# A two-layer network on one core: a third block of seven products in three feed-forward stages, with one of its weight sums added by transfers

## The chip, the cores and the metric

The kernel runs on one core of a Trainium2 chip. The metric is device time in microseconds (us) of one execution. The core's engines each run their own list of instructions in order and wait for one another through semaphores: TensorE (PE, matrix products, with its weight loads shown apart as PEld), VectorE (DVE), ScalarE (ACT), GpSimd (POOL) and SyncE (SP), which here issues the DMA transfers.

## The reference, cut to what matters

The kernel computes two layers over 256 tokens of width 1024, all in fp32. Each layer is a feed-forward part, a mixer, and a second feed-forward part, each followed by a residual sum and a layer norm:

```python
def swiglu(x, w_in, w_out):                     # w_in 1024 x 5632, w_out 2816 x 1024
    gate, up = jnp.split(x @ w_in, 2, axis=-1)
    return (jax.nn.silu(gate) * up) @ w_out

for layer in range(2):
    h = layer_norm(ALPHA * h + 0.5 * swiglu(h, ffn_w_in[layer, 0], ffn_w_out[layer, 0]), ...)
    h = layer_norm(ALPHA * h + mix(h), ...)     # layer 0: gated delta rule and state space; layer 1: sparse attention
    h = layer_norm(ALPHA * h + 0.5 * swiglu(h, ffn_w_in[layer, 1], ffn_w_out[layer, 1]), ...)
```

So there are six stages. Stages 1, 3, 4 and 6 are feed-forward, and these are what the change is about. Stage 2 is the hybrid mixer and stage 5 the sparse attention.

## The kernel before, in words

**Products.** An fp32 product is made of three TensorE products in the reduced type fp32r: a value is split into a high part (`hi`, a copy that rounds) and a low part (`lo`, the value less its high part), and hi·hi, hi·lo and lo·hi are summed (`mm3`). Weights come from DRAM into one of four `raw` buffers (128 partitions x 2048 values, 1 MB). ACT, sometimes DVE as a CAST, copies each half of it (128x1024) into a `whi` buffer, and DVE subtracts to make `wlo`. These, the results `g` and other intermediates such as `e` (128x1024) come from a pool of 36 buffers of one size, in which weights have a quota of 12 to 24. The activations of a stage lie in an `x` buffer of 128x4096 values (2 MB). There are two of these, so during a stage one of them is spare until the stage's layer norm writes the next stage's activations.

**A feed-forward stage.** The 2816 hidden columns are 11 steps of 256. The first step or two (`NT`) are done token by token. The rest follow a string, `PATTERN`, in which a letter stands for:

- R, one plain step (`proj_two`). Four banks (ps, ps, mp, mp) take 8 matmuls of 128x512 and 8 of 128x256 each: 32 and 32. DVE and ACT then add the two halves of each bank into `sg`, apply SiLU, multiply, and split the result into `g`.
- S, two steps at once (`block`), as a fast 2x2 block product with seven products instead of eight. Each product is 12 matmuls of 128x512, 84 in all. The left factors are blocks and sums of blocks of the activations (`sums_of_tokens`, made once for a stage, tiles `sgh` and `sgl`). The right factors are b11, b21, b22 and four weight sums T1 to T4, each in two halves h = 0 and 1 of 128x1024. T1 = b11 + b12, T3 = b12 + b22, T2 = T1 + b22 and T4 = T2 + b21, each added in place (T3 over b12, the others over b11); the signs lie in the activation sums. For each half DVE adds, then the sum is split into `whi` and `wlo` like any weight. Four banks A, B (tag ps) and C, D (tag mp) gather the products, `e1` and `e2` hold the partial results, and 8 transposes (128x128) bring the result into the form of `g`.

After each letter the out-projection of the step before goes into four `acc` banks: for a block 48 matmuls of 128x512.

Stage 1 (NT = 1) has the string "RRRSRSRR", and stages 3, 4 and 6 (NT = 2) have "RSRRSRR".

**Order.** The code writes operations in program order into a `Plan`. A list scheduler in it (`order`) decides the order of each engine's instructions, with a price for each operation, priorities, quotas and a table `ORDER` of corrections. So an edit of `block` moves instructions on every engine. All instructions are issued by one line (L559 before, L564 after), so profile rows are told apart by the names of their tiles. A number after a name in an order row says which tile it is.

Of the kernel before, what the change touches and what calls it, by code (L numbers as in the profile page):

```python
# [9 lines left out]
F32 = mybir.dt.float32  # L10
F32R = mybir.dt.float32r
I32 = mybir.dt.int32
AF = mybir.ActivationFunctionType
OP = mybir.AluOpType
# [18 lines left out]
    "ps": (2, "PSUM"), "mp": (2, "PSUM"), "acc": (4, "PSUM"),  # L33
}

QUOTAS = {"M": None, "S": (8, 8), "Z": (4, 4), "L": (4, 4), "G": (4, 4), "P": (5, 5), "Q": (5, 5), "D": (4, 4), "W": (12, 24)}

KEPT = ("L", "G")

# [6 lines left out]

KEEP_WARM = 5500

PATTERN = {1: "RRRSRSRR", 2: "RSRRSRR"}


def H3(t, h):
# [120 lines left out]
class Plan:  # L173
# [76 lines left out]
    def price(self, op, eng, fn, args, kw):  # L250
# [13 lines left out]
                return 63.0 if N <= 64 else max(146.0, N * 0.896)  # L264
            return N * 1.7708 if N > M else 235.0 if N == M else 224.0
        if fn == "dma_start":
            return 60.0
# [60 lines left out]
    def order(self, caps):  # L328
        ops = self.ops
        for op in ops:  # L330
            if op.fn == "dma_start":
                a = op.args[0] if isinstance(op.args[0], V) else op.args[1]
                op.nbytes = (a.p1 - a.p0) * a.ids.size * 4
                if isinstance(op.args[1], V) and op.args[1].t.space == "DRAM":
# [12 lines left out]
            op.table = self.TABLES.get(getattr(op.args[2], "name", str(op.args[2])) if op.fn == "activation" else "")  # L347
# [8 lines left out]
        ready = {e: [] for e in engs}  # L356
        free = {e: 0.0 for e in engs}
        table = None
        dma_free = 0.0
        partial = heavy = False  # L360
        run = 0
        last = None
# [68 lines left out]
        while left:  # L431
# [79 lines left out]
                port = st + c  # L511
            op.start = st
            if fn == "dma_start":
                dma_free = max(dma_free, st + 1300) + op.nbytes / 360.0
                op.end = dma_free + 600
                free[e] = st + c
            else:
                op.end = st + c
                free[e] = st + c
# [63 lines left out]
class K:  # L583
    NT = 2
    LAG = 5

    def __init__(self, plan, ins, caps):
        self.nc = self.plan = plan
# [327 lines left out]
    def block(self, st, w, c0, c1):  # L916

        nc, V = self.nc, self.nc.vector
        raw = []
        for h in range(2):  # L920
            tiles = [self.plan.tile("raw", [P, 2048], F32, "raw", stream="W") for r in range(2)]
            for r, t in enumerate(tiles):
                for e, c in enumerate((c0, c1)):
                    k = 4 * r + 2 * h
                    nc.sync.dma_start(t[:, e * 1024:(e + 1) * 1024].rearrange("p (k n) -> p k n", k=2),
                                      w[:, k:k + 2, c:c + 512])
            raw.append(tiles)
        A, B, C, D = (self.bank(tag) for tag in ("ps", "ps", "mp", "mp"))
        e1, e2 = self.m4(1024, "e1"), self.m4(1024, "e2")
        lh, rh = slice(0, 512), slice(512, 1024)  # L930

        def form(n, h):
            (r1, r2), u, v = raw[h], slice(0, 1024), slice(1024, 2048)
            left = r1[:, u]
            if n == "T1":
                V.tensor_tensor(left, left, r1[:, v], OP.add)
            elif n == "T3":
                V.tensor_tensor(r1[:, v], r1[:, v], r2[:, v], OP.add)
            elif n == "T2":
                V.tensor_tensor(left, left, r2[:, v], OP.add)  # L940
            elif n == "T4":
                V.tensor_tensor(left, left, r2[:, u], OP.add)
            src = {"b21": r2[:, u], "b22": r2[:, v], "T3": r1[:, v]}.get(n, left)
            hi, lo = self.m4(1024, "whi", "W", F32R), self.m4(1024, "wlo", "W", F32R)
            self.split(hi, lo, src)
            return hi, lo
# [6 lines left out]
                    self.mm3(bank, st[a][2 * h + k], (hi[:, cs], lo[:, cs]), start and h + k == 0, stop and h + k == 2,  # L953
                             **({} if start else {"skip_group_check": True}))
        product(A, "a11", "b11", True, True)
        product(B, "5", "T1", True, True)
        self.copy(e1[:, lh], A)
        product(A, "a12", "b21", False, True)
        self.copy(e1[:, rh], B)
        product(C, "7", "T3", True, True)  # L960
        nc.scalar.activation(e2[:, lh], A, AF.Silu)
        V.tensor_tensor(e1[:, rh], e1[:, rh], C, OP.subtract)
        product(B, "3", "b22", False, True)
        product(D, "2", "T2", True, True)
# [3 lines left out]
        V.tensor_tensor(e2[:, rh], B, e1[:, lh], OP.add)  # L968
        V.tensor_tensor(e2[:, lh], e2[:, lh], e2[:, rh], OP.mult)
        V.tensor_tensor(e1[:, rh], e1[:, rh], e1[:, lh], OP.add)  # L970
# [15 lines left out]
    def ffn(self, l, j, x, then):  # L986
# [62 lines left out]
        def flush(keep):  # L1049
            while len(todo) > keep:  # L1050
                f, g, wo = todo.pop(0)
                out_mm(0, f, g, wo)
                if f >= NF - self.LAG:
                    late.append((f, g, wo))
                else:
                    out_mm(1, f, g, wo)
        st = None
        s = NT
        for n, kind in enumerate(PATTERN[NT]):
            if n == 3:  # L1060
                self.mark = len(self.plan.ops) - 1
            if kind == "S":
                if st is None:
                    st = self.sums_of_tokens(x)
                go = self.block(st, w_in, s * 256, DFF + s * 256)
                next(go)
                wo = self.unit_rows(w_out, 2 * s, 2, 0, D) + self.unit_rows(w_out, 2 * s + 2, 2, 0, D)
# [6 lines left out]
            if s == NT:  # L1074
                for m in range(NT):
                    wo = self.unit_rows(w_out, 2 * m, 2, 0, D)
                    todo += [(2 * m + e, gts[2 * m + e], wo[e]) for e in range(2)]
# [1040 lines left out]
    def run(self, stages):  # L2118
# [53 lines left out]
SPLIT, SHIFT = 4900, 10  # L2172
HOMES = [38, 1389, 3572, 4905, 6238, 7367]
ORDER = {
# [98 lines left out]
```

## Time and profile before

| | us |
|---|---|
| runs (three) | 1091.36, 1091.8, 1095.76; median 1091.8 |
| profiled execution | 1091.2, with a span of 1089.5 |
| PE busy | 1076.1 (99%), 6132 matmuls |
| DVE busy | 968.5 (89%), 1471 instructions |
| ACT busy | 634.7 (58%), 1066 instructions |
| POOL busy | 49.1 (5%), 78 instructions |
| stage 1, hybrid mixer | 0 to 194, 197 to 424.7 |
| stages 3 and 4 | 424.7 to 605.3, 605.3 to 787.5 |
| sparse attention, stage 6 | 787.5 to 906.6, 906.6 to 1083.7 |

The span is what the profiler saw from the first to the last instruction; the profiled execution's own time is 1.7 us longer. The stages are cut at their layer norms. Matmuls are pipelined, so the mean of one matmul in a group of the page (390 ns) is longer than the pitch at which they follow each other. The prediction goes by pitches.

### The profile page before, as it was taken

To read this page: it belongs to the slowest core of one execution; us is meant where nothing else is said; L and a number is where in the kernel's file an instruction comes from. 1 tells how busy PE (TensorE), PEld (TensorE's weight loads), DVE (VectorE), ACT (ScalarE), POOL (GpSimd) and SP (SyncE) were. 2 spreads that over 40 slices of the span, in tenths; PEclk is the share of its full clock that TensorE was granted. 3 is DMA by queue.
4 is the path that set the end of the run, shared out by engine and by line. 5 is a ranking of instruction groups with operands and counts; after the bars stand their busy time and mean duration, and the time that the engine had idled before them with its cause. 6 is when DMAs were issued, how large, how long until landed. Compare 5 with 4: busy or idle time off the path is not lost.

```text
span 1089.5 us, 16005 instructions
## 1 busy us (share of the span) xinstructions
PE 1076.1 (99%) x6132; PEld 907.0 (83%) x6132; DVE 968.5 (89%) x1471; ACT 634.7 (58%) x1066; POOL 49.1 (5%) x78
## 2 busy tenths in 40 slices
PE   8999999999999999999999999999999999999997
PEld 6888888788999788888888888888887678888886
DVE  7999996888979899999995999897888999999965
ACT  5665673489788544555573655564375765655540
POOL 0000300001000110000000000010001000000000
PEclk9999999999999999999999999999999999999999
DMA  9919395633652383458394609378464145285541
GB/s 331 325 31 335 116 341 171 215 116 104 213 191 100 116 302 114 164 178 285 109 340 169 222 11 332 132 239 276 155 197 152 59 136 192 79 282 182 208 140 39
DMA packets 135799, 201.52 MB, mean 185 GB/s; under 512 B 10077, under 2 KB 95530, under 8 KB 135722
## 3 DMA queue, kind: packets, MB, share of 16 engines
q1 hardware_dynamic: 135722, 200.50, 54.2%
q8 instruction: 48, 0.79, 0.3%
q14 instruction: 29, 0.24, 0.1%
HBM read 197.18 MB, written 1.07 MB: 182 GB/s over the span
## 4 chain that ended last, share of the span: by engine, by line
PE 93%; DVE 3%; DMA 2%; ACT 1%; issue 1%; SPq 0%; DVEq 0%; ACTq 0%
PE ps L559 38%; PE acc L559 33%; PE mp L559 22%; DMA raw<-in_ffn_w_in_dram 1%; DVE arena L559 1%; DVE wlo L559 1%; DVE qs L559 0%; SPq L559 0%; DMA arena<-in_ssd_a_log_dram 0%; ACT whi L559 0%; DVE h L559 0%; DVE P L559 0%; DVE F L559 0%; ACT L559 0%; DVE g L559 0%
## 5 line engine op out<-in xcount | busy, mean ns | idle before, releaser
L559 DVE TENSOR_TENSOR wlo<-raw,whi 128x1024 fp32r<-128x1024 f32 (+1 forms) x396 | 469.0, 1213 | 10.2 <-ACT whi L559 7.7
L559 ACT ACTIVATE whi<-raw 128x1024 fp32r<-128x1024 f32 (+1 forms) x356 | 361.1, 1050 | 136.6 <-DMA raw<-in_ffn_w_in_dram 55.2
L559 PE MATMUL acc<-whi,g 128*128 128x512 f32 x704 | 223.3, 390 | 0.0
L559 PE MATMUL ps<-whi,x 128*128 128x512 f32 (+1 forms) x608 | 169.9, 386 | 1.3 <-DVE whi L559 1.3
L559 PE MATMUL ps<-x,whi 128*128 128x512 f32 (+1 forms) x720 | 159.2, 343 | 1.0 <-ACT cv L559 0.9
L559 PEld LDWEIGHTS acc<-whi,g 128*128 128x128 f32 x704 | 132.3, 188 | 26.7
L559 PE MATMUL acc<-wlo,g 128*128 128x512 f32 x352 | 137.4, 390 | 0.0
L559 PEld LDWEIGHTS ps<-x,whi 128*128 128x128 f32 x720 | 123.0, 189 | 17.2 <-ACT cv L559 2.4
L559 PEld LDWEIGHTS ps<-whi,x 128*128 128x128 f32 x608 | 109.7, 188 | 23.7 <-DVE whi L559 2.1
L559 PE MATMUL ps<-x,wlo 128*128 128x256 f32 x544 | 98.9, 284 | 0.0
L559 PE MATMUL ps<-wlo,x 128*128 128x512 f32 (+1 forms) x304 | 95.0, 385 | 0.5 <-DVE wlo L559 0.5
L559 PEld LDWEIGHTS ps<-x,wlo 128*128 128x128 f32 x544 | 81.1, 191 | 2.2 <-issue 0.2
L559 PE MATMUL mp<-x,whi 128*128 128x512 f32 x336 | 80.8, 390 | 0.2 <-DVE g L559 0.2
L559 ACT ACTIVATE sg<-ps 128x256 f32<-128x256 f32 x56 | 21.3, 380 | 95.6 <-PE ps L559 95.5
L559 PEld LDWEIGHTS acc<-wlo,g 128*128 128x128 f32 x352 | 66.2, 188 | 12.8
L559 PEld LDWEIGHTS mp<-x,whi 128*128 128x128 f32 x336 | 62.9, 188 | 13.6 <-DVE g L559 0.6
L559 DVE TENSOR_TENSOR sg<-ps,sg 128x256 f32<-128x256 f32 x56 | 23.4, 419 | 48.0 <-ACT sg L559 47.6
L559 PE MATMUL acc<-whi,x 128*128 128x512 f32 x192 | 65.3, 406 | 0.1
L559 PEld LDWEIGHTS ps<-wlo,x 128*128 128x128 f32 x304 | 55.5, 188 | 11.1 <-DVE wlo L559 1.0
L559 DVE TENSOR_TENSOR raw<-raw,raw 128x1024 f32<-128x1024 f32 x48 | 57.9, 1228 | 0.2
L559 PE MATMUL mp<-x,wlo 128*128 128x256 f32 x336 | 44.2, 283 | 0.0
L559 PEld LDWEIGHTS mp<-x,wlo 128*128 128x128 f32 x336 | 42.2, 192 | 0.2
(293 smaller groups left out, 1535.2 us busy)
## 6 DMA issues: line engine op xcount, KB each, us to landing
raw<-in_ffn_w_out_dram SPq DMA_DIRECT2D x44, 1024.0 KB, 5.0
raw<-in_ffn_w_in_dram SPq DMA_DIRECT2D x88, 512.0 KB, 5.3
raw<-in_ffn_w_in_dram SPq DMA_DIRECT2D x42, 1024.0 KB, 8.0
raw<-in_hyb_w_in_dram SPq DMA_DIRECT2D x20, 1024.0 KB, 6.0
raw<-in_hyb_w_out_dram SPq DMA_DIRECT2D x8, 1024.0 KB, 5.9
raw<-in_nsa_w_in_dram SPq DMA_DIRECT2D x5, 1024.0 KB, 5.9
raw<-in_nsa_w_out_dram SPq DMA_DIRECT2D x4, 1024.0 KB, 5.1
w<-in_nsa_cmp_w_dram SPq DMA_DIRECT2D x8, 512.0 KB, 9.0
```

Of the source, the lines that this page charges most:

```text
L559: r = getattr(getattr(nc, eng), fn)(*[res(a) for a in args], **{k: res(a) for k, a in kw.items()})
```

## The change

It has five parts.

1. In stages 3, 4 and 6 the string becomes "RSRSSR": five plain steps and two blocks become three plain steps and three blocks. Stage 1 keeps its string.
2. In every block of all four stages the seven products come in another order: b11, b22, b21, T1, T3, T2, T4 instead of b11, T1, b21, T3, b22, T2, T4. Two signs and one operation on `e` are rearranged for that; their number stays.
3. In stages 3, 4 and 6 the raw weights of half h = 1 of a block are loaded into the spare `x` buffer (`HOME`), by four transfers of 512 KB, and worked on there, instead of into two `raw` buffers.
4. In stages 3, 4 and 6 T3 is no longer added by DVE. GpSimd issues a transfer with an adding operation, SBUF to SBUF, 512 KB for each half (`BY_DMA`): 2 for a block, 18 in all. Before, GpSimd issued no transfer.
5. The planner gets prices for such transfers, and the table of corrections switches from one stage's entries to the next's 100 operations before the stage's end in stages 1 and 4 (`TAIL`), where it was at half of the stage. The order in the two mixers stays.

```diff
-PATTERN = {1: "RRRSRSRR", 2: "RSRRSRR"}
+PATTERN = ["RRRSRSRR", "RSRSSR", "RSRSSR", "RSRSSR"]
...
+    HOME = [("raw", "raw")] + [("raw", "x")] * 3
+    BY_DMA = [()] + [("T3",)] * 3
...
-            tiles = [self.plan.tile("raw", [P, 2048], F32, "raw", stream="W") for r in range(2)]
+            whole = None
+            if self.HOME[self.count][h] == "x":
+                whole = self.plan.tile("x", [P, 4096], F32, "x", stream="")
+            for r in range(2):
+                pair = whole[:, r * 2048:(r + 1) * 2048] if whole is not None else self.plan.tile("raw", ...)
...
+            to, more = {"T1": (left, right), "T3": (right, part["b22", h]), "T2": (left, part["b22", h]),
+                        "T4": (left, part["b21", h])}.get(n, (None, None))
+            if to is not None:
+                if n in self.BY_DMA[self.count]:
+                    nc.gpsimd.dma_start(to, more, accum_op=OP.add)
+                else:
+                    V.tensor_tensor(to, to, more, OP.add)
...
         product(A, "a11", "b11", True, True)
-        product(B, "5", "T1", True, True)
+        product(B, "3", "b22", True, True)
         self.copy(e1[:, lh], A)
         product(A, "a12", "b21", False, True)
         self.copy(e1[:, rh], B)
+        product(B, "5", "T1", False, True)
+        nc.scalar.activation(e2[:, lh], A, AF.Silu)
         product(C, "7", "T3", True, True)
-        nc.scalar.activation(e2[:, lh], A, AF.Silu)
-        V.tensor_tensor(e1[:, rh], e1[:, rh], C, OP.subtract)
-        product(B, "3", "b22", False, True)
+        V.tensor_tensor(e1[:, rh], e1[:, rh], C, OP.add)
         product(D, "2", "T2", True, True)
...
-                if n + 1 in (1, 4) and op.idx >= (marks[n] + marks[n + 1]) // 2:
+                if n + 1 in (1, 4) and op.idx >= marks[n + 1] - TAIL:
```

On PE, in stage 3, this is one of the two plain steps R that stand behind the second block before (its last transposes first):

```order
L559 MATMUL mp_5488<-ident_130,e_869_5355 128x128 x4
L559 MATMUL mp_5493<-ident_130,e_860_5312 128x128 x4
L559 MATMUL ps_5502<-x_4289,whi_5427 128x512 x8
L559 MATMUL ps_5521<-x_4289,whi_5451 128x512 x8
L559 MATMUL mp_5536<-x_4289,whi_5435 128x512 x8
L559 MATMUL mp_5552<-x_4289,whi_5458 128x512 x8
L559 MATMUL ps_5502<-x_4289,wlo_5460 128x256 x8
L559 MATMUL ps_5521<-x_4289,wlo_5485 128x256 x8
L559 MATMUL mp_5536<-x_4289,wlo_5468 128x256 x8
L559 MATMUL mp_5552<-x_4289,wlo_5500 128x256 x8
```

Two such steps go and a third block comes. Within it, on PE after, this is where T1's product (bank ps_5385) ends and T3's (mp_5446, whose weights are the sum that the transfer made) begins:

```order
L564 MATMUL ps_5385<-wlo_5420,sgh_4586 128x512
L564 MATMUL ps_5385<-whi_5409,sgl_4601 128x512
L564 MATMUL acc_4659<-whi_5231,g_5362 128x512
L564 MATMUL mp_5446<-whi_5437,sgh_4586 128x512
L564 MATMUL acc_4659<-wlo_5238,g_5362 128x512
L564 MATMUL acc_4659<-whi_5231,g_5372 128x512
L564 MATMUL acc_4667<-whi_5231,g_5362 128x512
L564 MATMUL acc_4667<-wlo_5238,g_5362 128x512
L564 MATMUL mp_5446<-wlo_5443,sgh_4586 128x512
L564 MATMUL mp_5446<-whi_5437,sgl_4601 128x512
```

The scheduler has put five matmuls of the out-projection between the first two of T3's product, so PE reads T3's `whi` of half 0 one matmul after T1's product, and its `wlo` five matmuls later.

On DVE before, this is the part of the second block of stage 3 in which weight sums are made (`raw<-raw` adds within one buffer, `raw<-raw,raw` adds from another; raw_5027 is half 0 and raw_5108 half 1):

```order
L559 TENSOR_TENSOR raw_5027<-raw_5027 128x1024
L559 TENSOR_TENSOR wlo_5147<-raw_5108,whi_5136 128x1024
L559 TENSOR_TENSOR raw_5027<-raw_5027,raw_5063 128x1024
L559 TENSOR_TENSOR wlo_5164<-raw_5027,whi_5151 128x1024
L559 TENSOR_TENSOR raw_5108<-raw_5108 128x1024
L559 TENSOR_TENSOR raw_5027<-raw_5027,raw_5063 128x1024
L559 TENSOR_TENSOR raw_5108<-raw_5108,raw_5128 128x1024
L559 TENSOR_TENSOR wlo_5193<-raw_5108,whi_5180 128x1024
L559 TENSOR_TENSOR raw_5108<-raw_5108,raw_5128 128x1024
```

On DVE after, the same part of the third block of stage 3, where raw_5200 is half 0 and x_5261 half 1:

```order
L564 TENSOR_TENSOR raw_5200<-raw_5200 128x1024
L564 TENSOR_TENSOR x_5261<-x_5261 128x1024
L564 COPY e_881_5387<-ps_5385 128x512
L564 TENSOR_TENSOR wlo_5413<-raw_5200,whi_5400 128x1024
L564 TENSOR_TENSOR wlo_5420<-x_5261,whi_5409 128x1024
L564 TENSOR_TENSOR raw_5200<-raw_5200,raw_5221 128x1024
L564 TENSOR_TENSOR x_5261<-x_5261 128x1024
L564 TENSOR_TENSOR wlo_5443<-raw_5200,whi_5437 128x1024
L564 CAST whi_5454<-x_5261 128x1024
L564 TENSOR_TENSOR wlo_5463<-raw_5200,whi_5456 128x1024
```

The first two rows are T1's adds, which read b12. The rows on wlo_5413 and wlo_5420 split T1, and the next two are T2's adds. T3's add is gone from here: wlo_5443 splits T3's half 0 and whi_5454 copies its half 1, and between T1's adds and these rows the transfers must be issued and land.

Also on DVE after, this is the end of the second block of stage 3, whose x buffer (x_4855) must be free before the third block's loads into x_5261 may start:

```order
L564 CAST whi_5229<-x_4855 128x1024
L564 TENSOR_TENSOR wlo_5238<-raw_4987,whi_5231 128x1024
L564 TENSOR_TENSOR wlo_5248<-x_4855,whi_5229 128x1024
L564 TENSOR_TENSOR wlo_5259<-raw_4987,whi_5233 128x1024
L564 TENSOR_TENSOR e_838_5173<-e_838_5173,mp_5243 128x512
L564 TENSOR_TENSOR wlo_5277<-raw_5008,whi_5241 128x1024
L564 TENSOR_TENSOR wlo_5284<-raw_5008,whi_5250 128x1024
L564 TENSOR_TENSOR e_838_5173<-mp_5269,e_838_5173 128x512
L564 TENSOR_TENSOR wlo_5299<-raw_5200,whi_5256 128x1024
L564 TENSOR_TENSOR e_846_5216<-ps_5171,e_838_5173 128x512
L564 TENSOR_TENSOR wlo_5312<-x_5261,whi_5291 128x1024
```

The row on wlo_5248 is the last reader of the second block's half, and the last row is the first use on DVE of the third block's half (its ACT copy whi_5291 comes before it). Seven rows stand between.

On POOL after, in stage 3, the six adding transfers stand between the small power operations of the layer norms. Before, no row stood between these:

```order
L564 TENSOR_TENSOR lnve_4369<-lnve_4369,mhalf_110 128x1
L564 DMA raw_4481<-raw_4527 128x1024
L564 DMA x_4324<-x_4324 128x1024
L564 DMA raw_4908<-raw_4941 128x1024
L564 DMA x_4855<-x_4855 128x1024
L564 DMA raw_5200<-raw_5221 128x1024
L564 DMA x_5261<-x_5261 128x1024
L564 TENSOR_TENSOR lnve_5817<-lnve_5817,mhalf_110 128x1
```

The two transfers of a block are issued one behind the other, each once T1's add of its half is done.

More of the change, by code (lines that the diff above doesn't have):

```diff
@@ L34 @@
 }
-QUOTAS = {"M": None, "S": (8, 8), "Z": (4, 4), "L": (4, 4), "G": (4, 4), "P": (5, 5), "Q": (5, 5), "D": (4, 4), "W": (12, 24)}
+QUOTAS = {"M": None, "S": (8, 8), "Z": (4, 4), "L": (4, 4), "G": (4, 4), "P": (5, 5), "Q": (5, 5), "D": (4, 4), "W": (12, 24), "R": (8, 8)}
 KEPT = ("L", "G")
@@ L266, in price @@
         if fn == "dma_start":
-            return 60.0
+            return 1000.0 if eng == "gpsimd" else 60.0
         N = n(args[0]) if isinstance(args[0], V) else n(args[1])
@@ L333, in order @@
                 op.nbytes = (a.p1 - a.p0) * a.ids.size * 4
-                if isinstance(op.args[1], V) and op.args[1].t.space == "DRAM":
+                if isinstance(op.args[1], V) and (op.args[1].t.space == "DRAM" or op.eng == "gpsimd"):
                     op.nbytes *= 2
@@ L358, in order @@
         table = None
-        dma_free = 0.0
+        dma_free = add_free = 0.0
         partial = heavy = False
@@ L513, in order @@
             if fn == "dma_start":
-                dma_free = max(dma_free, st + 1300) + op.nbytes / 360.0
-                op.end = dma_free + 600
+                if e == "gpsimd":
+                    add_free = max(add_free, st + 1300) + op.nbytes / (220.0 if dma_free > st else 360.0)
+                    dma_free += op.nbytes / 360.0
+                    op.end = add_free + 600
+                else:
+                    dma_free = max(dma_free, st + 1300) + op.nbytes / 360.0
+                    op.end = dma_free + 600
                 free[e] = st + c
@@ L918, in block @@
         nc, V = self.nc, self.nc.vector
-        raw = []
+        part = {}
         for h in range(2):
-            tiles = [self.plan.tile("raw", [P, 2048], F32, "raw", stream="W") for r in range(2)]
-            for r, t in enumerate(tiles):
+            whole = None
+            if self.HOME[self.count][h] == "x":
+                whole = self.plan.tile("x", [P, 4096], F32, "x", stream="")
+            for r in range(2):
+                pair = whole[:, r * 2048:(r + 1) * 2048] if whole is not None else self.plan.tile("raw", [P, 2048], F32, "raw", stream="W")
                 for e, c in enumerate((c0, c1)):
                     k = 4 * r + 2 * h
-                    nc.sync.dma_start(t[:, e * 1024:(e + 1) * 1024].rearrange("p (k n) -> p k n", k=2),
-                                      w[:, k:k + 2, c:c + 512])
-            raw.append(tiles)
+                    t = pair[:, e * 1024:(e + 1) * 1024]
+                    nc.sync.dma_start(t.rearrange("p (k n) -> p k n", k=2), w[:, k:k + 2, c:c + 512])
+                    part["b%d%d" % (r + 1, e + 1), h] = t
         A, B, C, D = (self.bank(tag) for tag in ("ps", "ps", "mp", "mp"))
@@ L932, in form @@
         def form(n, h):
[L933 to L943, printed above, removed]
+            left, right = part["b11", h], part["b12", h]
+            to, more = {"T1": (left, right), "T3": (right, part["b22", h]), "T2": (left, part["b22", h]),
[3 more added lines that the diff above has]
+                    nc.gpsimd.dma_start(to, more, accum_op=OP.add)
+                else:
+                    V.tensor_tensor(to, to, more, OP.add)
+            src = part.get((n, h), right if n == "T3" else left)
             hi, lo = self.m4(1024, "whi", "W", F32R), self.m4(1024, "wlo", "W", F32R)
@@ L968, in block @@
         V.tensor_tensor(e2[:, rh], B, e1[:, lh], OP.add)
+        V.tensor_tensor(e1[:, rh], e2[:, rh], e1[:, rh], OP.subtract)
         V.tensor_tensor(e2[:, lh], e2[:, lh], e2[:, rh], OP.mult)
-        V.tensor_tensor(e1[:, rh], e1[:, rh], e1[:, lh], OP.add)
         V.tensor_tensor(e1[:, lh], C, e1[:, lh], OP.subtract)
@@ L1056, in flush, with first @@
                     out_mm(1, f, g, wo)
+        def first():
+            for m in range(NT):
+                wo = self.unit_rows(w_out, 2 * m, 2, 0, D)
+                todo.extend((2 * m + e, gts[2 * m + e], wo[e]) for e in range(2))
         st = None
         s = NT
-        for n, kind in enumerate(PATTERN[NT]):
+        self.count = getattr(self, "count", -1) + 1
+        for n, kind in enumerate(PATTERN[self.count]):
             if n == 3:
@@ L1066, in ffn @@
                 next(go)
+                if n == 0:
+                    first()
                 wo = self.unit_rows(w_out, 2 * s, 2, 0, D) + self.unit_rows(w_out, 2 * s + 2, 2, 0, D)
@@ L1073, in ffn @@
             wu = self.unit_cols(w_in, DFF + s * 256, 256)
[L1074 to L1077, printed above, removed]
+            if n == 0:
+                first()
             banks = self.proj_two(x, (wg[0], wu[0], wg[1], wu[1]), ("ps", "ps", "mp", "mp"))
@@ L2172 @@
 SPLIT, SHIFT = 4900, 10
+TAIL = 100
 HOMES = [38, 1389, 3572, 4905, 6238, 7367]
```

## The prediction, made before the changed kernel was run

> **What bounds the kernel now.** I read the page's busy times first, then the chain that ended last, then the stages.
>
> ```profile
> PE 1076.1 (99%) x6132; PEld 907.0 (83%) x6132; DVE 968.5 (89%) x1471; ACT 634.7 (58%) x1066; POOL 49.1 (5%) x78
> ...
> PE 93%; DVE 3%; DMA 2%; ACT 1%; issue 1%; SPq 0%; DVEq 0%; ACTq 0%
> ```
>
> ```profile
> 424.70:605.30 180.60, 180.60 (x892) 152.49 (x891) 165.63 (x217) 94.54 (x135) 1.85 (x2) 1.00 0.59 201
> 605.30:787.50 182.20, 182.20 (x917) 154.88 (x916) 163.17 (x230) 101.07 (x149) 7.31 (x20) 1.00 0.59 200
> 906.60:1083.70 177.10, 175.38 (x864) 148.08 (x863) 150.73 (x196) 85.13 (x127) 3.21 (x3) 1.00 0.45 158
> ...
> DVE sg L559 <- ACT sg L559: 11.1, 5, 10.2
> ...
> DVE sg L559 <- ACT sg L559: 10.8, 5, 8.8
> ...
> DVE sg L559 <- ACT sg L559: 17.8, 4, 15.2
> ```
>
> The three window rows are stages 3, 4 and 6: length, then PE, PEld, DVE, ACT and POOL busy, the granted clock (1.00) and the DMA share. PE is busy for all of the first two, so a matmul saved there is time saved, as long as nothing makes PE wait. DVE comes next: it is idle for 180.60 - 165.63 = 15.0, 19.0 and 26.4 us. The last three rows are the waits of DVE in the same stages. Most of its idle time, 11.1, 10.8 and 17.8 us, is one long wait near the stage's end for PE's last products. Before that DVE hardly rests.
>
> **PE: blocks for plain steps.** These are stretches of the timeline of PE in stage 3: start, length, tile, count. First one R, then one S, then half of an S's transposes.
>
> ```profile
> 513.06 3.63 PE ps L559 x16
> 516.69 3.63 PE mp L559 x16
> 520.31 1.91 PE ps L559 x16
> 522.23 1.92 PE mp L559 x16
> ...
> 465.61 8.16 PE ps L559 x36
> 473.77 2.72 PE mp L559 x12
> 476.49 2.72 PE ps L559 x12
> 479.21 5.44 PE mp L559 x24
> ...
> 489.93 0.60 PE L559 MATMUL mp<-ident,e 128*128 128x128 f32 x4
> 490.28 3.00 PE L559 MATMUL ps<-x,whi 128*128 128x512 f32 x12
> ```
>
> R is 11.09 us. S is 19.04, or 84 matmuls at 2.72/12 = 0.227, and its 8 transposes take 2 x 0.35 (490.28 - 489.93). Two R are 22.18 and one S with transposes 19.74, so a stage loses 2.44 us of PE. The out-projections are the same. Three stages: -7.3 us. The new order of products in all blocks, stage 1 included, changes no count, and I cost it at nothing because the same splits stand ahead of the same number of matmuls.
>
> **DVE: what the third block adds.** Instructions in an unbroken run follow each other at a pitch shorter than their own duration; (length - one duration)/(count - 1) is the pitch.
>
> ```profile
> 467.20 5.76 DVE L559 TENSOR_TENSOR wlo<-raw,whi 128x1024 fp32r<-128x1024 f32 x5
> 463.79 3.49 DVE L559 TENSOR_TENSOR raw<-raw,raw 128x1024 f32<-128x1024 f32 x3
> 456.38 0.75 DVE L559 TENSOR_TENSOR sg<-mp,sg 128x256 f32<-128x256 f32 x2
> 459.18 1.29 DVE L559 CAST whi<-raw 128x1024 fp32r<-128x1024 f32 x2
> 488.31 1.28 DVE L559 TENSOR_TENSOR e<-e 128x512 f32<-128x512 f32 x2
> ```
>
> Splits and adds go at 1.14, 512-wide `e` operations and 1024-wide casts at 0.60, 256-wide `sg` operations at 0.33. By the counts of the two orders a later stage gains 6 splits (+6.8), 2 adds (18 for 16; +2.3) and 7 `e` operations (+4.2), and loses 12 `sg` and `g` operations (-4.0): +9.3, less or more with the copies that go to ACT or DVE. With these it is +6.5, +10.0 and +9.5 in the three stages. Left on DVE, T3 would be 6 adds a stage, 6.8 us more. Idle time left is 15.0 - 6.5 - 2.4 = 6.1, then 19.0 - 10.0 - 2.4 = 6.6, then 14.4 us. On the sum DVE still fits, but without slack at the places where it must be early.
>
> **How early DVE is.** Near the end of stage 3's first block DVE finishes a split of T4 and PE reads it later:
>
> ```profile
> 480.24 1.23 DVE L559 TENSOR_TENSOR wlo<-raw,whi 128x1024 fp32r<-128x1024 f32 x1
> ...
> 481.76 0.39 PE L559 MATMUL mp<-whi,x 128*128 128x512 f32 x1
> 482.90 0.61 PE L559 MATMUL mp<-whi,x 128*128 128x512 f32 x2
> ```
>
> DVE ends at 481.47 and the matmul that needs it begins after 482.90 (483.12 by the pitch): 1.65 us ahead. I laid both orders out with the pitches above, from the stage's first product. Up to that split DVE has 86.4 us of work before and PE 67.2, a difference of 19.2. Up to the third block's T4 after, it is 152.3 and 133.9, or 18.4. So DVE would be 1.65 + 0.8 = 2.5 us ahead, less some 1.5 us in which it must wait for the second block's products: about 1.0 us in stage 3, and by the same count 1.2 and 1.3 in stages 4 and 6. At the first block of stage 3 it is 1.9, elsewhere 2.5 or more.
>
> **The adding transfer.** In the third block of stage 3, seven DVE rows stand between T1's add of half 0 and T3's split: 5 at 1.14 and one `e` at 0.60, or 6.3, less 1.2 for the ACT copy with its semaphores (copies follow at 1.05): 5.1 us. The same count gives 5.2 in stage 4 and 4.5 in stage 6; half 1 has 6.3, 6.6 and 5.7. With DVE's lead, a transfer may take 6.1, 6.4 and 5.8 us from T1's add to its landing at no cost. Each microsecond more is about one of PE in each of three blocks; beyond 6.4 the first block of stage 3 joins (window 4.5). No row shows such a transfer. The nearest:
>
> ```profile
> 465.05 3.15 ACT L559 ACTIVATE whi<-raw 128x1024 fp32r<-128x1024 f32 x3 [5.02 <-DVE raw L559]
> ...
> Y<-zeros SPq DMA_DIRECT2D x2, 512.0 KB, 3.8
> raw<-in_ffn_w_in_dram SPq DMA_DIRECT2D x88, 512.0 KB, 5.3
> raw<-in_ffn_w_out_dram SPq DMA_DIRECT2D x44, 1024.0 KB, 5.0
> raw<-in_ffn_w_in_dram SPq DMA_DIRECT2D x42, 1024.0 KB, 8.0
> ...
> DMA to landing us min/median/max: 3.5/5.4/10.9
> ...
> L559 POOL TENSOR_TENSOR lnve<-lnve,mhalf x12: 921/956/995, 184.4 to 1084.0; 128x1 f32<-128x1 f32 x12
> ```
>
> The lower end is 3.8 us, the plain copy of 512 KB within SBUF: then the transfers cost nothing. The upper end is 10.9, the slowest load of a `raw` tile: (10.9 - 6.1) x 3 plus 4.5 at the first block and the queue's second half is about 22 us. A gain by the transfer itself is excluded, since the DVE time that it saves is counted above. I take about 5.9: the copy's 3.8, some 1 us for POOL's instruction (the power row, 0.956, the nearest thing POOL does) and 1 us for reading the destination as well, an estimate from the 1024 KB loads, which took no longer than the 512 KB ones where they met little (5.0 to 5.3) and 8.0 where they met much. That is 0.1 us too late in stage 6, and nothing elsewhere. The Trainium skill's "DMA: Bandwidth & Descriptors", section on the anatomy of one DMA, fits 2.0 us plus the bytes at 436 GB/s; an estimate by it is 3.2 us for 512 KB and 4.4 for twice that, and the sum would then be the full -7.3.
>
> On POOL, the adds stand ahead of the attention's constants in stage 4 (7.31 us of POOL there), which are needed only in the stage that follows. The layer norms' power operations follow the adds of a stage and need not wait for them.
>
> **The x buffer.** In the third block the four loads into `x` start when the second block's last reader is done. By DVE's order 6.36 us of work stand between that reader and the first use, less 1.2 for ACT, plus the lead: 6.2 us until the first 512 KB must be there. The 512 KB row has 5.3: no cost. At the crowded row's 8.0 it is 1.8 us in each stage, 5.4 in all. The first block's loads stand on SP ahead of `w_out` loads and can push one of these back; I put 1 us in all for this and for ACT's extra waits. Before, at the same places, `raw` buffers gave PE only one wait of note:
>
> ```profile
> PE ps L559 <- DVE whi L559: 1.3, 1, 1.3
> ```
>
> Sum: -7.3 + 0.1 + 1.0 = -6.2. Against the profiled execution's 1091.2 that is 1085.0; its median stands 0.6 higher at 1091.8, so 1085.6. What a measurement here can tell from no change is about 0.5%, or 5.5 us: faster is below 1086.3, slower above 1097.3.
>
> **Rivals.**
> 1. *Transfers land late*, adds at 7 to 8 us or `x` at 8. For it: windows of 4.5 to 5.2 us and a lead of 1 leave no room, and other loads are in flight for 59% of the DMA engines' time. Against it: the median loads are inside. At X = 7 the cost is 0.9 + 0.6 + 1.2, with 0.6 at stage 3's first block: 3.3; at X = 8 it is 7. The time is 1088 to 1092.
> 2. *DVE becomes the bound.* If the long waits at the stage ends (11.1, 10.8, 17.8) stay whole, since DVE has nothing to do there, DVE's work plus these is more than the stage: 11.1 - 6.1 = 5.0, 10.8 - 6.6 = 4.2 and 17.8 - 14.4 = 3.4, together 12.6. The time is 1091.8 - 7.3 + 12.6 = 1097, or less where a part of the waits goes. Against it: DVE that comes later waits less at the end, and my count up to the third block leaves it 1 us ahead.
> 3. *Slower: POOL cannot start the transfers while DVE runs.* Then an add goes out only when DVE stops for want of it, and of the 5.9 us all but the lead of 1.0 is in the open: 4.9 in each third block, about 3.5 at the first block of stage 3: +18, less 7.3, gives 1102. It decides from about X = 8. Against it: the twelve POOL power rows take 921 to 995 ns, spread over the whole span, beside a DVE that is busy 89%, so POOL's own work isn't held up. But that is arithmetic; no row shows POOL issuing a transfer. A rule behind this rival: the Trainium skill's "SBUF — State Buffer", section on the two separate sides, says that GpSimd cannot write a transfer's descriptors while VectorE holds the port that they share, and gives about 3100 ns instead of 620 beside a copy. By that rule copies hold it, and additions of two SBUF inputs do only against GpSimd instructions that read SBUF; the DVE rows in these windows are nearly all of the second kind, so here it speaks less against the change than its figure does. My chance goes by the POOL rows.
> 4. *The third block brings nothing*, as its products start late by more than 2.4 us in each stage for another reason (banks, `g` buffers): 1090 to 1093, inside the first rival's time.
>
> **Chances.** The forecast (1083.5 to 1087) 0.50, of which some 0.04 lies above 1086.3; rival 1 with 4, 0.22; rival 2, 0.14, of which a third passes 1097.3; rival 3, 0.10; and 0.04 for something that makes it faster than 1083.5. Faster: 0.46 + 0.04 = 0.50; slower: 0.10 + 0.05 = 0.15; same: 0.35. To hold 8 in 10 the range runs from 1083.5, which is all of PE's saving and a little over, to 1096, which takes in rival 1 and most of rival 2.
>
> **What would show it.** Right: windows of stages 3, 4 and 6 about 2 us shorter each with PE still busy for all of them; 18 POOL transfers of 512 KB that land within 6 us; DVE's long wait at the stage ends shrunk by some 5 to 9 us. Wrong: waits of PE for `whi` or `wlo` in the third blocks, and behind them ACT or DVE waiting for a transfer on `raw` or `x`. If the add's landing is above 7 us, the term of the transfers has failed; if it is below 6 and PE waits for DVE splits, the lead has; if PE is dense and the stages aren't shorter, the pitch has.

## The result: 6 us faster, and the profile after

The changed kernel takes 1085.92 us (median of 14 runs, 1085.0 to 1093.18) where the kernel before takes 1092.69 beside it (14 runs, 1090.34 to 1096.85). The ratio is 0.9945, with a 95% interval of 0.9928 to 0.9962, or 6.0 us. On two later occasions it was 0.9928 (0.9906 to 0.9949) and 0.9946 (0.9933 to 0.9959).

The first lines of the page of the changed kernel's first profile, and its rows for the transfers that GpSimd issues:

```profile
PE 1074.1 (99%) x6024; PEld 900.4 (83%) x6024; DVE 994.2 (91%) x1474; ACT 647.3 (59%) x1054; POOL 68.6 (6%) x96
...
PE 86%; DVE 8%; DMA 2%; issue 2%; ACT 1%; POOL 1%; SPq 0%; DVEq 0%; POOLq 0%; ACTq 0%
...
raw<-raw POOLq DMA_DIRECT2D x9, 512.0 KB, 4.7
x<-x POOLq DMA_DIRECT2D x9, 512.0 KB, 5.4
```

PE has 6132 - 6024 = 108 matmuls fewer: 192 of 128x256 less, 60 of 128x512 and 24 transposes more. DVE has gone from 89% to 91% although it issues as many instructions, and its share of the chain from 3% to 8%: PE is still the bound, but DVE now reaches into it. In that first profile 25 us of the hybrid mixer ran at a granted clock of 0.86, which made the mixer 4.4 us longer; so stages are read from the second profile of the same kernel (span 1085.1), in which this didn't happen (those 25 us have 1.00 there). Windows cut at the layer norms: first three of the kernel before (stages 3, 4, 6), then the six stages of the changed kernel. Columns as in the prediction.

```profile
425.03:605.59 180.56, 180.56 (x892) 152.45 (x891) 165.59 (x217) 94.54 (x135) 1.85 (x2) 1.00 0.59 201
605.59:787.77 182.18, 182.18 (x918) 154.85 (x917) 163.12 (x230) 101.07 (x149) 7.31 (x20) 1.00 0.59 200
906.79:1084.02 177.23, 175.19 (x864) 147.93 (x862) 150.84 (x196) 85.13 (x127) 3.22 (x4) 1.00 0.45 158
```

```profile
0.00:194.45 194.45, 191.59 (x937) 159.47 (x938) 175.76 (x229) 114.74 (x157) 15.85 (x21) 1.00 0.68 231
194.45:425.21 230.76, 229.63 (x1800) 201.50 (x1799) 203.94 (x398) 156.22 (x275) 16.34 (x10) 1.00 0.51 167
425.21:603.55 178.34, 178.34 (x856) 149.28 (x855) 171.45 (x211) 103.40 (x138) 7.31 (x8) 1.00 0.70 232
603.55:784.62 181.07, 180.74 (x882) 151.41 (x881) 172.14 (x234) 102.56 (x142) 13.54 (x27) 1.00 0.65 207
784.62:903.65 119.03, 117.60 (x731) 90.85 (x730) 108.08 (x205) 81.65 (x221) 7.29 (x21) 1.00 0.44 144
903.65:1079.34 175.69, 173.32 (x827) 144.67 (x826) 160.40 (x199) 88.65 (x121) 8.44 (x10) 1.00 0.54 176
```

Stage 3 is 2.2 us shorter, stage 4 1.1 and stage 6 1.5: 4.9 of the 7.3 us of work that PE has less. Stages 1, 2 and 5 have their lengths of before within 0.15 us. DVE's busy time grew by 5.9, 9.0 and 9.6 us in the three stages.

Where did 2.4 us stay? Third block of stage 6, second profile, timeline: GpSimd's two issues, T1's add of half 1 on DVE, and then DVE and PE at the place where half 1 is awaited (start, length; in brackets the idle time before a row, and what ended it):

```profile
1022.65 0.86 POOL L564 DMA_DIRECT2D raw<-raw  x1 [37.96 <-DVE raw L564]
1023.79 0.85 POOL L564 DMA_DIRECT2D x<-x  x1 [0.28 <-issue]
...
1022.03 1.22 DVE L564 TENSOR_TENSOR x<-x 128x1024 f32<-128x1024 f32 x1
...
1028.32 1.23 DVE L564 TENSOR_TENSOR wlo<-raw,whi 128x1024 fp32r<-128x1024 f32 x1 [0.44 <-ACT whi L564]
1031.26 0.69 DVE L564 CAST whi<-x 128x1024 fp32r<-128x1024 f32 x1 [1.71 <-DMA x<-x]
...
1032.01 0.73 PE L564 MATMUL mp<-whi,sgh 128*128 128x512 f32 x2 [0.33 <-DVE whi L564]
```

The transfers of these two issues, with the time from issue to landing:

```profile
raw<-raw POOLq DMA_DIRECT2D x1, 512.0 KB, 4.6
...
x<-x POOLq DMA_DIRECT2D x1, 512.0 KB, 7.4
```

Half 0 lands 4.6 us after its issue. Half 1, issued 1.1 us later while half 0 is in flight, takes 7.4 and lands at 1031.2, 7.9 us after T1's add of it (1022.03 + 1.22). DVE stands still for 1.71 us, uses up its lead, and PE waits: its next matmul comes 0.73 us behind the one at 1031.28 instead of 0.227. So about 0.5 of the 0.9 us that stage 6 lost lies here.

Why does half 1 take so long? Two windows of the same profile and a line of its DMA queues between 1027 and 1031.2:

```profile
1024.00:1029.40 5.40, 5.40 (x25) 4.47 (x24) 4.96 (x5) 3.60 (x6) 0.64 (x1) 1.00 1.03 194
1029.50:1030.90 1.40, 1.40 (x8) 1.17 (x7) 0.05 (x1) 0.69 (x1) 0.00 (x0) 1.00 0.06 12
...
q8 instruction: 1, 0.02, 1.4%
```

The last two figures of a window are the busy share of the 16 DMA engines and GB/s. No load is in flight here, yet up to 1029.4 all engines are busy (1.03) and move 194 GB/s: the two adding transfers alone fill them, one after the other. From 1029.5 on the share is 0.06, one engine of 16. The trace's packet times show what that one did (they don't name the engine, but its packets follow one another without a gap): at 1027.93 it took a packet of 16 KB from the queue of instructions, which lasted 0.95 us, and its last packets of half 1 end at 1030.9, 1.4 us behind those of the other fifteen. The same is seen in the other two profiles of this kernel, with 7.4 us each time. By the other fifteen half 1 would have landed in about 6.0 us, an estimate; in stage 4, where no such packet fell into it, it took 6.1.

In stage 4 the loss is elsewhere: behind the third block ACT waits for the first load of the attention's weights with SiLU's work queued behind it, DVE for ACT, PE for `g`:

```profile
759.32 0.91 ACT L564 ACTIVATE whi<-raw 128x840 fp32r<-128x840 f32 x1 [1.54 <-DMA raw<-in_nsa_w_in_dram]
...
760.53 0.43 DVE L564 TENSOR_TENSOR sg<-mp,sg 128x256 f32<-128x256 f32 x1 [1.62 <-ACT sg L564]
...
766.80 0.50 PE L564 MATMUL acc<-whi,g 128*128 128x512 f32 x1 [0.33 <-DVE g L564]
...
727.35 0.49 DVE L564 CAST fixed<-mz 128x512 fp32r<-128x512 f32 x1 [0.74 <-POOL mz L564]
```

The last row is one that I had waved away: in the third block of stage 4 DVE waits 0.74 us for a constant that GpSimd makes after the adding transfers. By the distances between PE's matmuls the stop at 766.80 costs about 0.6 of the 1.3 us that stage 4 lost, and another 0.3 us go between 728.8 and 731.1, soon after that wait; the rest is in pieces of 0.1 us or less that weren't traced.

### The profile page after: what moved, and what is told of

Its sections match the earlier page's. It is cut to its first block, busy times and chain, and to the rows that moved or that the text cites. A ratio compares the mean times of both kernels' runs of the same rounds, so it can differ in the third digit from the quotient of the medians.

```text
span 1089.1 us, 15914 instructions
## 1 busy us (share of the span) xinstructions
PE 1074.1 (99%) x6024; PEld 900.4 (83%) x6024; DVE 994.2 (91%) x1474; ACT 647.3 (59%) x1054; POOL 68.6 (6%) x96
## 4 chain that ended last, share of the span: by engine, by line
PE 86%; DVE 8%; DMA 2%; issue 2%; ACT 1%; POOL 1%; SPq 0%; DVEq 0%; POOLq 0%; ACTq 0%
PE ps L564 36%; PE acc L564 31%; PE mp L564 19%; DVE wlo L564 4%; DVE e L564 1%; DVE arena L564 1%; DMA x<-x 1%; DMA raw<-in_nsa_w_in_dram 1%; DMA raw<-in_ffn_w_in_dram 0%; DVE qs L564 0%; ACT whi L564 0%; DVE g L564 0%; POOL arena L564 0%; DVE raw L564 0%; DVE x L564 0%
## 5 line engine op out<-in xcount | busy, mean ns | idle before, releaser
L564 DVE TENSOR_TENSOR wlo<-raw,whi 128x1024 fp32r<-128x1024 f32 (+1 forms) x351 | 418.5, 1212 | 8.9 <-ACT whi L564 6.7
L564 ACT ACTIVATE whi<-raw 128x1024 fp32r<-128x1024 f32 (+1 forms) x323 | 326.9, 1048 | 102.2 <-DVE raw L564 30.4
L564 PE MATMUL ps<-x,whi 128*128 128x256 f32 (+1 forms) x624 | 138.5, 338 | 1.0 <-ACT cv L564 0.9
L564 PEld LDWEIGHTS ps<-x,whi 128*128 128x128 f32 x624 | 106.4, 192 | 13.5 <-ACT cv L564 2.4
L564 DVE TENSOR_TENSOR wlo<-x,whi 128x1024 fp32r<-128x1024 f32 x63 | 76.3, 1217 | 0.0
L564 ACT ACTIVATE whi<-x 128x1024 fp32r<-128x1024 f32 x54 | 56.7, 1053 | 30.5 <-DMA x<-in_ffn_w_in_dram 10.5
L564 PE MATMUL mp<-x,whi 128*128 128x512 f32 x240 | 58.6, 391 | 0.0
L564 PEld LDWEIGHTS mp<-x,whi 128*128 128x128 f32 x240 | 44.8, 188 | 9.3
L564 ACT ACTIVATE e<-ps 128x512 f32<-128x512 f32 x30 | 17.9, 597 | 43.2 <-PE ps L564 43.0
L564 PEld LDWEIGHTS acc<-whi,x 128*128 128x128 f32 x192 | 35.4, 188 | 8.1 <-DVE q L564 0.8
```

What stands on the lines that cost most here:

```text
L564: r = getattr(getattr(nc, eng), fn)(*[res(a) for a in args], **{k: res(a) for k, a in kw.items()})
```

## The experiments

### What the parts are worth

Theory: PE is the bound, so the gain is the third block's matmuls; the transfers and the x buffer only keep DVE and the loads early enough. Rivals: the gain comes from the order or the relief of DVE; the transfers aren't needed.

**again**: the changed kernel itself.

> The changed kernel itself, for a second profile and to be timed beside the others. If its gain is PE's (7.3 us of matmuls less, given back in part by waits in the later blocks), the time is 1085 to 1087 again, stages 3, 4 and 6 are shorter than before by about 2.2, 1.0 and 1.5 us, and the hybrid mixer has its length of before (230.7 us), since the 4.4 us that it had more in the first profile went with a granted clock of 0.86 in 25 us of it. If the mixer really is slower after the change, it has 235 us again.

1086.43 us (1085.97 to 1088.8). It is the second profile shown above: the mixer has its old length, and the stages are as expected.

**old_strings**: the strings of before, all else new.

```diff
-PATTERN = ["RRRSRSRR", "RSRSSR", "RSRSSR", "RSRSSR"]
+PATTERN = ["RRRSRSRR", "RSRRSRR", "RSRRSRR", "RSRRSRR"]
```

> The strings of before (RSRRSRR in stages 3, 4 and 6), with the new order of products, the x buffer for half 1, and the adding transfers kept. Theory (the gain is the third block's saving on PE): PE has the matmuls of before, so 1090.5 to 1092.5, level with the kernel before. Rival (the gain comes from the order, the buffers or the relief of DVE): 1085 to 1088.

1091.27 us, ratio 0.9977 (0.9959 to 0.9994): 0.2% below the kernel before, with an interval that ends just under 1. Its profile says it more sharply:

```profile
426.03:606.50 180.47, 180.47 (x892) 152.43 (x891) 157.71 (x207) 99.38 (x141) 5.56 (x7) 1.00 0.68 223
606.50:788.62 182.12, 182.12 (x918) 154.97 (x917) 158.49 (x227) 100.21 (x148) 15.06 (x24) 1.00 0.62 200
907.59:1085.13 177.54, 175.48 (x863) 147.84 (x862) 145.28 (x191) 86.74 (x128) 6.72 (x7) 1.00 0.52 169
```

DVE has 4.6 to 7.9 us less to do than before, and the stages are as long as before to 0.3 us. So in these stages relief of DVE alone buys nothing; the third block's matmuls are the gain.

**t3_on_dve**: each adding transfer replaced, at its place, by DVE's add; no other instruction changes its place.

```diff
-    nc.gpsimd.dma_start(to, more, accum_op=OP.add)
+    nc.vector.tensor_tensor(to, to, more, OP.add)      # put in when the finished order is written out
```

> T3 is added by DVE at the place where the transfer was issued; every other instruction of every engine stands in the same order as in the changed kernel. Theory (the transfers pay because DVE has no slack): 6 adds of 1.14 us a stage more on DVE, of which PE sees all but the lead of about 1 us at each third block and what is idle at the stage's end: 3 to 5 us in stage 3, 2 to 4 in stages 4 and 6, so 1093 to 1098. Rival (DVE is off the path, the transfers are not needed): 1085 to 1088.

1097.08 us, ratio to before 1.0033 (1.0015 to 1.0052): 10.7 us slower than the changed kernel.

```profile
429.00:611.96 182.96, 179.61 (x856) 148.90 (x855) 177.63 (x217) 103.30 (x138) 1.84 (x3) 1.00 0.59 209
611.96:796.53 184.57, 181.51 (x882) 151.22 (x881) 178.84 (x240) 103.11 (x142) 10.99 (x20) 1.00 0.54 186
915.52:1093.15 177.63, 174.43 (x828) 144.47 (x826) 166.54 (x205) 88.75 (x121) 3.22 (x3) 1.00 0.44 157
```

The stages are 4.6, 3.5 and 1.9 us longer for 6.1 to 6.7 us more of DVE: PE sees most of it in stage 3, where DVE had least idle time, and least in stage 6. In this order of instructions the third block pays only with the transfers; an order planned afresh with these adds on DVE wasn't run.

**raw_home**: half 1 in raw buffers, as before.

```diff
-    HOME = [("raw", "raw")] + [("raw", "x")] * 3
+    HOME = [("raw", "raw")] * 4
```

> The changed kernel with the raw weights of half 1 in two raw buffers, as before, in place of the spare x buffer; the planner orders it anew. Theory (the x buffer is needed because a third block that follows the second would have to wait for raw buffers, of which there are four and a block takes all): loads of the third block and of the output weights beside it come some us late, 2 to 4 us a stage, 1091 to 1098. Rival (only the strings and the transfers count): 1085 to 1088.

1107.01 us, ratio 1.0130 (1.0111 to 1.0149), worse than expected. Stages 3, 4 and 6 are 3.8, 8.6 and 4.8 us longer than the changed kernel's, and the attention, which wasn't edited, 4.4. In stage 3 the wait of ACT for loads of input weights, all of them into `raw` here, is 18.1 us, where the changed kernel has 5.9 for `raw` and 5.2 for `x`, 11.1 together, and PE waits 3.4 us for a copy by ACT:

```profile
ACT whi L564 <- DMA raw<-in_ffn_w_in_dram: 18.1, 11, 3.8
...
PE ps L564 <- ACT whi L564: 3.4, 1, 3.4
```

That ACT waits longer for loads without the x buffer is shown. How much of the rest is the planner's new order isn't, and a part of it may be the clock: stage 4 has a granted clock of 0.96 in this profile, 1.00 in the changed kernel's.

### How much room the transfers have

**late_adds**: GpSimd is held for a while before the issue; every other instruction keeps its place.

```diff
+                if eng == "gpsimd" and fn == "dma_start" and args[0].t.tag == "raw":
+                    nc.gpsimd.tensor_copy(idle[:, 0:1], T1_of_half_0[:, 0:1])
+                    for _ in range(4):
+                        nc.gpsimd.memset(idle, 0.0)
```

> The changed kernel with every other instruction in the same order, but GpSimd is held, after T1's add of half 0, by a 128x1 copy and four memsets of 128x512 (0.54 us each by the profile) before it issues a block's transfers: both land about 2.5 us later. Theory (the window plus DVE's lead of about 1 us is used up in the third blocks): no cost in the second blocks, about 1.5 to 2.5 us in each third block and 0 to 1.5 in the first block of stage 3, so 1090 to 1094. Rival (the transfers are hidden with room to spare): 1085 to 1087.

1101.3 us, ratio 1.0058 (1.0037 to 1.0079): 15 us slower than the changed kernel, about twice the most that I expected. GpSimd's rows at the first and the third block of stage 3:

```profile
459.28 4.52 POOL L565 COPY idle<-raw 128x1 f32<-128x1 f32 x1 [33.89 <-DVE raw L568]
463.86 2.28 POOL L567 MEMSET idle<- 128x512 f32 x4
466.36 1.09 POOL L568 DMA_DIRECT2D raw<-raw  x1 [0.22 <-issue]
...
547.02 1.06 POOL L565 COPY idle<-raw 128x1 f32<-128x1 f32 x1 [35.12 <-DVE raw L568]
548.14 2.28 POOL L567 MEMSET idle<- 128x512 f32 x4
550.59 0.87 POOL L568 DMA_DIRECT2D raw<-raw  x1 [0.17 <-issue]
```

The copy of one column took 4.52 us at the first block, and stage 3 lost 9.1 us there and later; more on that copy stands at the end. Stages 4 and 6 are the cleaner test. There the third block's issue of half 0 came 3.2 us later in the stage than in the changed kernel (120.47 for 117.26 us after the stage's start, and 122.21 for 119.00), and the stages got 2.33 and 2.27 us longer. PE has one long wait in each, 2.4 and 2.7 us, for ACT's copy of the sum. If every microsecond beyond the room that half 0 has costs one, as the prediction has it, that room is about 0.9 us in a third block. One delay alone can't show this slope, and in stage 6 half 1 was late already without it. The delays of the first two blocks cost next to nothing there: PE has no long wait at them.

### The order of the products, and a better kernel

**old_products**: the seven products in the order of before.

```diff
-        product(B, "3", "b22", True, True)      # b11, b22, b21, T1, T3, T2, T4
+        product(B, "5", "T1", True, True)       # b11, T1, b21, T3, b22, T2, T4
...
```

> The changed kernel with the seven products in the order of before (T1 second, T3 fourth), everything else kept; the planner orders it anew. By its order the transfer of the third block of stage 3 has 7.5 us of DVE work between T1's add and T3's split where the changed kernel has 6.3. Theory (what counts is the window, and the new order of products isn't part of the gain): 1085 to 1088. Rival (the new order of products is needed for the gain): above 1090.

1085.39 us, ratio 0.9934 (0.9921 to 0.9948). Run again beside the changed kernel:

> The changed kernel once more, only to be compared with the next one on the same chip: 1085 to 1087.

> The strings, the x buffer and T3's transfers of the changed kernel with the products in the order of before, once more beside it. In the first profile its stages 4 and 6 were 1.1 and 0.7 us shorter than the changed kernel's. If the longer window is worth that, it is 1 to 2.5 us faster than the changed kernel run beside it, 1083.5 to 1085.5; if the difference was chance, level within 0.5 us.

The changed kernel takes 1086.26 us (six runs, 1085.48 to 1086.64), this one 1084.1 (six runs, 1083.71 to 1088.54, five of them below 1085.1): 2.2 us less, and 0.9935 (0.9918 to 0.9952) of the kernel before. It beats both kernels. Its windows:

```profile
424.36:602.60 178.24, 178.24 (x856) 149.33 (x855) 172.50 (x214) 100.33 (x135) 7.54 (x9) 1.00 0.70 232
602.60:782.48 179.88, 179.88 (x882) 151.75 (x881) 171.71 (x233) 103.00 (x143) 13.71 (x26) 1.00 0.65 209
901.49:1076.45 174.96, 172.93 (x827) 144.81 (x826) 160.48 (x199) 87.58 (x121) 8.40 (x9) 1.00 0.54 177
```

They are 2.32, 2.30 and 2.27 us shorter than before: 6.9 of the 7.3. DVE is as busy as in the changed kernel, to about a microsecond, and PE is busy for all of stages 3 and 4. In this order T1 is the second product and T3 the fourth, and T3's split stands further behind T1's add; DVE has no wait for a transfer in stage 6. The new order of products, with the order of instructions that the planner makes of it, is no part of the gain, it costs some 2 us. That the longer window does it fits stage 6, but there half 1 also landed in 6.2 us instead of 7.4, since no packet of instructions fell into its transfer, and the two weren't separated; in stage 4, where the loss was behind the attention's loads, the first of these loads is issued 1.3 us earlier in this kernel's stage, and what counted wasn't separated.

**old_products_tail**: with the old place of the switch in the planner's table as well.

```diff
-                if n + 1 in (1, 4) and op.idx >= marks[n + 1] - TAIL:
+                if n + 1 in (1, 4) and op.idx >= (marks[n] + marks[n + 1]) // 2:
```

> As the one before, with the planner's corrections of the next stage beginning at half of stages 1 and 4, as before the change, instead of 100 operations before their end. Theory (this part only reorders what has slack): level within 1 us. Rival (the stage boundary's order mattered): 2 us or more slower, seen in stages 4 and 5.

1108.36 us, ratio 1.0161 (1.0140 to 1.0181): 24 us slower than without this line. Stage 4 is 180.56 us, with PE busy for only 175.11, the attention 136.69 where it has 119.01, and stage 6 177.41 for 174.96. The rival holds: with these strings the old switch gives the end of stage 4 and the start of the attention another order, in which DVE comes late. It was tried with the old order of products only.

**old_t2** and **old_t2_stage1**: on top of old_products T2 by transfers too, and a third block in stage 1 as well.

```diff
-    BY_DMA = [()] + [("T3",)] * 3
+    BY_DMA = [()] + [("T3", "T2")] * 3
```

> As the one before (products in the order of before), and T2 is added by transfers as well as T3 in stages 3, 4 and 6: 18 more transfers, 6.8 us of DVE less in each of the three stages. Theory (about 2.2 of the 7.3 us are lost to DVE and ACT running late in the third blocks): the relief wins a part of it back, 1084 to 1086. Rival (what is lost has other causes, such as loads): 1086 to 1088. If T2's transfers land late, which its own split would show: above 1089.

> As the one before, and stage 1 also gets a third block: RRSRSSR for RRRSRSRR, with its half 1 in the spare x buffer and T2 and T3 by transfers there too. PE loses another 2.44 us; DVE in stage 1 was busy for 176 of 194 us. Theory (PE is the bound wherever DVE has its lead): 1 to 2.5 us less than the one before, 1081.5 to 1085. Rival (stage 1, with its start waiting for the first loads, has no lead to spare): no gain or a loss, 1085 to 1090.

1098.54 us, ratio 1.0055 (1.0043 to 1.0067), and 1113.23 us, 1.0183 (1.0170 to 1.0196), with 207.77 us for stage 1. In old_t2 DVE has less to do (169.68 us for 172.50 in stage 3) and yet stage 3 is 3.2 us longer than in old_products, stage 4 2.3, stage 6 0.5, and the attention 6.3. The four transfers of the third block of stage 4, in the order of their issue (at 722.02, 723.16, 725.42 and 726.70 us):

```profile
raw<-raw POOLq DMA_DIRECT2D x1, 512.0 KB, 4.7
...
x<-x POOLq DMA_DIRECT2D x1, 512.0 KB, 6.3
...
raw<-raw POOLq DMA_DIRECT2D x1, 512.0 KB, 7.8
...
x<-x POOLq DMA_DIRECT2D x1, 512.0 KB, 9.0
```

Transfers in flight together lengthen each other, and T2's are the last ones in line. ACT waits 1.2 us for the last of these four, which is the third alternative of the expectation. How much of the stages' loss goes back to it isn't shown: in stage 3 the timeline has no wait of ACT or DVE for one of the transfers, and PE's one long wait, 2.2 us, is for an `e` of DVE. The 6.3 us of the attention aren't explained by late transfers either; its order came out differently, as in raw_home.

**old_stage1**: as old_products, with the third block in stage 1 by T3's transfers alone.

```diff
-PATTERN = ["RRRSRSRR", "RSRSSR", "RSRSSR", "RSRSSR"]
+PATTERN = ["RRSRSSR", "RSRSSR", "RSRSSR", "RSRSSR"]
...
-    HOME = [("raw", "raw")] + [("raw", "x")] * 3
-    BY_DMA = [()] + [("T3",)] * 3
+    HOME = [("raw", "x")] * 4
+    BY_DMA = [("T3",)] * 4
```

> As old_products_b, and stage 1 gets a third block, RRSRSSR, with its half 1 in the spare x buffer and T3 by transfers. PE loses 2.44 us of 191; DVE gains about 9 us of work, 183 of then 191.5. Theory (a third block pays where DVE keeps its lead; here the first loads take it): the stage doesn't get shorter, or gets longer by some us, as with T2 by transfers, where it was 14 us longer: 1085 to 1095. Rival (T2's transfers alone made that loss): 1081 to 1084.

1088.71 us, ratio 0.9963 (0.9947 to 0.9978). Stage 1 takes 196.14 us with the third block and 193.59 without, and DVE's busy time in it rises from 174.78 to 186.34. There the third block doesn't pay, as the theory has it; that it is the first loads that take DVE's lead there wasn't traced.

## Why the prediction was right, and where it was lucky

The forecast was -6.2 us, 1085.6; the measured ratio makes it -6.0.

- **PE's term** (-7.3) holds: old_products has 6.9 of it, and old_strings, without the third block, nothing. DVE's added work was forecast as 6.5, 10.0 and 9.5 us and is 5.9, 9.0 and 9.6.
- **The lead** of about 1 us at the third blocks holds. In stage 6 DVE's copy would have been ready at 1030.24 without the wait of 1.71 us, 1.27 ahead of PE's turn at 1031.51; the forecast for that stage was 1.3. In late_adds window and lead less the landing of half 0 come out as 0.9, by the forecast's slope of one for one. It was the number on which most rested.
- **The adding transfer**: 5.9 us were forecast from T1's add to the landing. Half 0 took about 5.1 to 5.4 in the third blocks (4.6 to 4.9 after an issue that begins some 0.5 us after the add). Half 1 was mis-sized: it takes 5.9 to 7.4 us from its issue there, since half 0 fills the DMA engines ahead of it, which I counted only as a place in GpSimd's queue. From the add it is 6.8, 6.6 and 7.9 us, where I had allowed 7.3, 7.8 and 7.0 (window and lead): only stage 6 lost by it, and there 1.4 of the 7.9 were a packet of instructions that I had not thought of.
- **The x buffer** was forecast at no cost in the third block, with 6.2 us for the first load. That load landed 4.0 to 4.1 us after its issue in all three stages; ACT waits 3.0 to 3.1 us for it and 2.0 for another, but PE doesn't wait. Where the prediction says that shorter transfers would make the sum the full -7.3, it leaves out the 1.0 that it puts in for loads and ACT's waits: -6.3.
- **"0.1 + 1.0"** for the waits was less than half of what it should have been: 2.4 us by the second profile. Its places were the third blocks and what stands behind them, not the first block's loads. By the spans of the profiles before and after (the second) the gain is 4.4 us, and by the runs 6.0 with an interval from 4.2 to 7.9; that the sum met the median is in part luck.
- **The signs**: 15 of the 18 transfers land within 6 us, and stage 3 is about 2 us shorter as it should be, stages 4 and 6 less. One of the signs of wrong showed too, in the third block of stage 6: PE waits for `whi`, and behind it DVE for a transfer on `x`.
- **DVE's long waits at the stage ends** shrank, so the second rival fell. In stage 3 and 6 of the second profile:

```profile
DVE sg L564 <- ACT sg L564: 0.5, 2, 0.2
...
DVE sg L564 <- ACT sg L564: 2.1, 3, 1.0
```

  They were 11.1 and 17.8, and so shrank by more than the 5 to 9 us that were forecast; in stage 6 the wait for `acc` at the layer norm grew from 3.3 to 7.3 us.
- **The first rival** (late transfers) is what the loss in stage 6 is, with one transfer late by about 1 us instead of all. In late_adds a delay of 3.2 us cost 2.3 in each third block of stages 4 and 6, which fits the price of one for one behind some room.
- **The third rival** (GpSimd can't start transfers beside DVE) fell: the 18 issues took 0.85 to 1.1 us beside a DVE that was busy 96% of stage 3. By the rule of the Trainium skill that stood beside it ("SBUF — State Buffer", on the two separate sides), additions of two SBUF inputs don't hold up descriptors; the trace agrees, with those numbers.
- **"Costed at nothing"**: the order of products cost about 2 us and was no part of the gain. The place of the switch in the planner's table isn't nothing either: with the old place and the old order of products the kernel is 24 us slower (old_products_tail); with the new order this wasn't run. The constants of the attention on GpSimd were used in stage 4 already and cost DVE 0.74 us.

## What to carry to other kernels

Where one engine is dense and the next one has little idle time, work can be taken from the dense one by giving more to the other, but only together with the means that keep it ahead at the place where it is needed: alone, the relief bought nothing (old_strings) and the third block lost some 3 us against the kernel before (t3_on_dve). Ask of each asynchronous step how many microseconds of other work stand between its start and its first reader, plus the reader's lead; here that sum less the landing time was about 0.9 us, and a delay of 3.2 us made a stage 2.3 longer. Two steps that are issued close together also wait for each other: ask for the landing of the second one. Try the edit's parts one by one: one of them, the new order of products, cost 2 us of the gain, and a setting of the planner that looked like bookkeeping was worth 24, as far as it was tried.

## What the runs showed of the hardware that I had not expected

- An adding transfer of 512 KB within SBUF, issued by GpSimd, lands 4.5 to 5.3 us after its issue in the changed kernel when no other is in flight (up to 6.2 in old_products_b, beside loads). Two of them keep all 16 DMA engines busy at about 194 GB/s, 2.7 us for each, so a second one issued 1.1 to 1.5 us behind the first took 5.9 to 7.4, and of four issued within 5 us the last took 9.0. A plain copy that fills as much of SBUF, from a tile of zeros, took 3.8.
- One packet of 16 KB from the queue of instructions, 0.95 us on one DMA engine, made a transfer that is spread over 16 engines land 1.4 us later, in the same place in three profiles.
- GpSimd's copy of 128x1 out of SBUF took 0.18 to 4.52 us in late_adds. The 4.52 us lie beside DVE's rows that subtract or add two SBUF inputs without a gap, and it ended at 463.80, with the first gap in them:

```profile
459.13 1.22 DVE L568 TENSOR_TENSOR wlo<-raw,whi 128x1024 fp32r<-128x1024 f32 x1
460.26 1.22 DVE L568 TENSOR_TENSOR wlo<-x,whi 128x1024 fp32r<-128x1024 f32 x1
461.40 1.22 DVE L568 TENSOR_TENSOR wlo<-raw,whi 128x1024 fp32r<-128x1024 f32 x1
462.54 1.22 DVE L568 TENSOR_TENSOR x<-x 128x1024 f32<-128x1024 f32 x1
463.83 1.23 DVE L568 TENSOR_TENSOR raw<-raw,raw 128x1024 f32<-128x1024 f32 x1
```

  The Trainium skill, in the same section, says that such operations of VectorE keep out a GpSimd instruction that reads SBUF. This row agrees, with four of them on end; the issue of a transfer and a memset were not held up.
